# First layer's normed x transposed in one go ahead of its columns, x first in the load order, c read from two rows, other scheduling numbers

## The chip, the core and the metric

The kernel runs on one core of a Trainium2 chip. Its engines are named as the profile names them: PE (TensorE's matmuls; PEld its weight loads), DVE (VectorE), ACT (ScalarE), POOL (GpSimd, unused here), and SP (SyncE, which issues nearly all DMAs). The metric is the device time of one execution in microseconds (us); lower is better.

## What is computed

Two layers of an encoder over x (256 tokens x 2048 channels, float32), with a conditioning vector c of 2048 numbers:

```python
def hybrid_layer(x, c, ...):
    mod = (c @ w_ada + b_ada)[:, None, :]
    shift, scale, gate = jnp.split(mod, 3, axis=-1)
    h = rms_norm(x, g_pre) * (1 + scale) + shift
    z = h @ w_in                      # 2048 x 6144: u, g_pool, q, k, v, g_diff
    pool_out = multiscale_pool(u, w_pool, pool_scale) * jax.nn.silu(g_pool)
    q, k = apply_rope(q), apply_rope(k)
    att = rms_norm(diff_attention(q, k, v, lam), subln_g) * (1.0 - lam_init)
    diff_out = att * jax.nn.silu(g_diff)
    y = jnp.concatenate([pool_out, diff_out], axis=-1) @ w_out   # 2048 x 2048
    return x + (1 + gate) * rms_norm(y, g_post)
```

Everything is float32. Weights are 245 MB in all, read once.

## The kernel before

**Products.** The 256 tokens are two groups (st = 0, 1) of 128; the 2048 channels are 16 k tiles of 128, taken in pairs kp = 0..7. A *unit* is one 512 KB piece of w_in or w_out: two k tiles by 512 columns (one of the twelve column blocks nb of w_in). Most products split each float32 operand into a rounded part and a remainder: `whi` (ACT's CAST of the raw tile), `wlo` (DVE's subtraction), `hz` (both parts of h). A unit is then 12 matmuls. As k tiles of h become available one after the other, a column block is visited several times; at the end of a visit its sums are copied out to `z` and, at the next visit, back in to an accumulator bank.

**The start.** The modulation columns are needed before any h. DVE multiplies each 512 KB tile of w_ada (`adaz`, 128 channels by half of c) by c, which has been spread over all partitions (`cb`), and adds up along the row. Four such tiles give shift and scale of one k tile; three small steps write them to `AB`. c is spread by PE: `spread_c` multiplies a row of ones by c in four pieces (`psb<-cb,ones`), and ACT copies each to `cb`. Meanwhile x's two groups are squared and summed (`first_squares`), and `rms` gives each token's factor `ry`.

The first three units (group 1) are not split: full float32 products with the raw tiles (`accc<-rawz,halfz`), kp = 0 alone, in the order k0 of group 0, k0 of group 1, then k1 of both. Their h is made in `half_h`: ACT scales 256 columns of x by `ry`, PE transposes them (a matmul with the identity, `psb<-consts,halfz`), ACT applies `AB` and writes `halfz`. `half_h` also issues 18 dummy transposes (WARM) behind the first two. From the fourth unit on, the split products run without a pause: the main stream. For kp = 1..7 of the first layer `make_h` does the same as `half_h` when the k pair is due: two scalings, four transposes, four modulations from the PSUM bank, two subtractions.

**The order of the work.** The program is straight-line code for every engine, in an order that a planner sets while the kernel is built. Each part of the work is a task (`spawn`) with a due time; `Flow` keeps a model clock for each engine, with costs by operation (COST), by megabyte on the link (MB_US) and for landing (LANDING). `next_of` picks, for an engine, the task with the earliest due time that could start without idling; on PE a task with a due time counts as startable only SLACK us after its data is modelled ready. An engine executes its instructions strictly in this order, so an instruction that waits holds all behind it. `plan` fixes which unit follows which; ORDERS says which column block takes which place, RATE how many w_ada tiles are read per unit. The DMA issues wait on eight landing semaphores in turn, so at most eight loads are outstanding.

**Buffers.** PSUM has eight banks, four for sums (`accc`) and four others (`psb`); two of the second four hold the third first unit's sums (`accb`) through the start. `big` is a pool of 42 SBUF buffers of 4 KB per partition.

Of the kernel before, what the change touches and what calls it, by code (L numbers as in the profile page):

```python
# [129 lines left out]
class Flow:  # L130
# [10 lines left out]
    MB_US, LANDING, FIRST = 0.38, 2.4, 2.2  # L141
    COLD = (1.8, 4.0)

    SLACK = 1.5
# [66 lines left out]
    def next_of(self, k, asks):  # L211

        rows = []
        for t in asks:
            a = t.ask
            if a.dep is None:
                a.dep = self.depends(a)
            us = a.us + self.TABLE_US * bool(a.table and a.table[0] != self.table)
            due = t.due()
            slack = self.SLACK * (k == "tensor" and 0 < due < 1e8)  # L220
            rows.append((due, max(self.now[k], a.dep + slack), us, t))
# [29 lines left out]
    def turn(self, key, op, outs, ins, total, table):  # L251
# [8 lines left out]
        a.names = {r[0] for r in a.outs + a.ins} | {r[0] for _, r in a.also}  # L260
        a.dep, a.f32 = None, key == "tensor" and op == "matmul" and ins[-1].dtype == F32
# [143 lines left out]
class Kern:  # L405
# [169 lines left out]
    def run(self):  # L575
# [11 lines left out]
        self.rope_made = False  # L587
# [4 lines left out]
    def begin(self):  # L592
        nc, a, f = self.nc, self.a, self.f
        self.cb = self.const([P, D], "cb")
        nc.sync.dma_start(self.cb[0:1, :], a["c"])
        consts = self.const([P, HALF + P], "consts")
        nc.scalar.dma_start(consts, a["consts"])
        self.invf, self.ident = consts[:, :HALF], consts[:, HALF:]
        self.pos_i = self.const([P, NST], "posi", I32)
        nc.sync.dma_start(self.pos_i, a["positions"])  # L600
        self.cols = self.const([P, DEPTH, 89], "cols")
        nc.scalar.dma_start(self.cols, a["cols"])
        self.x = [self.const([P, D], f"x{st}_") for st in range(NST)]
# [4 lines left out]
        self.ones = self.const([1, P], "ones")  # L608
# [5 lines left out]
        self.arrived, self.squared = [False] * NST, False  # L614
        f.spawn(self.first_loads, -95.0)
        f.spawn(self.spread_c, -90.0)
# [13 lines left out]
        for l in range(DEPTH):  # L630
            f.spawn(lambda l=l: self.load_pool_weights(l))
            for kp in range(8):
                f.spawn(lambda l=l, kp=kp: self.make_h(l, kp), self.need_h(l, kp, 4.0))

    def first_loads(self):
# [13 lines left out]
        x(0)  # L649
# [11 lines left out]
    def spread_c(self):  # L661

        nc = self.nc
        for j in range(4):
            b, c = self.bank(), self.cb[:, j * 512 : (j + 1) * 512]
            nc.tensor.matmul(b, self.ones, c[0:1, :], start=True, stop=True)
            if j == 2:

                self.f.wait(lambda: self.squared)
            nc.scalar.copy(c, b)  # L670
            self.banks.give(b)
# [186 lines left out]
    def ada(self):  # L858

        v = self.nc.vector  # L860
        for e in self.adas:
# [9 lines left out]
            if i and 16 <= nt < 32 and (nt % 2 or not l and nt < 18):  # L871

                kt = nt - 16
                self.ab(l, kt if not l and kt < 2 else kt - 1, kt + 1)
# [4 lines left out]
    def ab(self, l, k0, k1):  # L879
# [5 lines left out]
        v.tensor_tensor(ab[:, 1], ab[:, 1], self.cols[:, l, 48 + k0 : 48 + k1], op=ALU.mult)  # L885

# [19 lines left out]
    def first_squares(self, st):  # L906
# [6 lines left out]
        if st:  # L913

            f.wait(lambda: self.made[0])
            more = self.big.take([P, D // 2], "junk")
            self.nc.vector.scalar_tensor_tensor(
                more, x[:, c[1]], self.ROOT**2, x[:, c[1]], op0=ALU.mult, op1=ALU.mult, accum_out=ss[:, st, 3:4]
            )
            self.big.give(more)  # L920
            f.wait(lambda: (0, 0) in self.h_whole)
            square(0)
        else:
            square(0), square(1)
# [3 lines left out]
        self.xr[0][st] = self.rms(ss[:, st, 2:5])  # L928
# [10 lines left out]
    def make_h(self, l, kp):  # L939
# [15 lines left out]
        f.wait(lambda: all(r is not None for r in self.xr[l]))  # L955
        xn = self.tmp.take([P, NST, S], "xn")
        for st in range(NST):
            self.scaled(xn[:, st, :], self.x[st][:, kp * S : (kp + 1) * S], self.xr[l][st])
# [524 lines left out]
```

## Time and profile before

| | us |
|---|---|
| median of 3 runs | 818.13 (816.19 to 821.13) |
| the profiled execution | 817.44 |
| its span, first to last instruction | 815.7 |
| PE busy in the span | 794.2 |
| first product of the first units | 15.84 |
| first product of the main stream | 31.25 |
| last product | 807.47 |

The span is 1.7 us shorter than the execution's time, which in turn is 0.7 us below the median. DVE is busy for 697.3 us, ACT for 545.8 us. The link moves 343 to 410 GB/s through the first 120 us, and less later. In the rows, a line gives the start, the duration, the engine, the source line, the operation, `out<-in` by tile names, the shape, and in brackets the idle time of the engine before it and what ended it. All work is recorded under line 125, a helper that records each operation, so the rows are read by tile names.

### The profile page before, as it was taken

What the parts mean: (1) busy time and instruction counts of PE and PEld (TensorE: products, weight loads), DVE (VectorE), ACT (ScalarE), POOL (GpSimd) and SP (SyncE); (2) the same over time, 40 slices, a digit from 0 to 9 for tenths busy, and PEclk for the clock granted to TensorE, in tenths of its full rate; (3) what the DMA queues carried; (4) which work ended last, traced back from release to release, by engine and by line L of the source; (5) the groups of instructions that cost most, each with busy time, mean ns of one, the idle gap of its engine ahead of it and who ended that gap; (6) DMA issues with size and microseconds to landing.
All of it is one profiled execution on the core that took longest, in us unless ns stands there. A gap on an engine that the chain in (4) does not pass through costs nothing. (4 is left out here: it accounts for less than half of the span.)

```text
span 815.7 us, 11813 instructions
## 1 busy us (share of the span) xinstructions
PE 794.2 (97%) x4032; PEld 658.5 (81%) x4032; DVE 697.3 (85%) x1232; ACT 545.8 (67%) x971; POOL 0.2 (0%) x4
## 2 busy tenths in 40 slices
PE   7899999999999999999999999999999999999995
PEld 3588789888997878788888889898898897787884
DVE  7889999998888899899999989878799889877924
ACT  4679998786655586886387557666656467677721
POOL 0000000000000000000000000000000000000000
PEclk9999999999999999999999999999999999999998
DMA  8999998999999877767999889999999895456302
GB/s 344 406 410 408 408 409 284 371 383 372 348 366 334 295 226 239 249 205 251 336 344 358 283 306 384 336 380 334 327 373 395 298 328 187 143 164 211 118 1 103
DMA packets 68382, 245.06 MB, mean 300 GB/s; under 512 B 7745, under 2 KB 8033, under 8 KB 68065
## 3 DMA queue, kind: packets, MB, share of 16 engines
q1 hardware_dynamic: 68034, 244.14, 82.6%
q8 instruction: 31, 0.51, 0.2%
q10 hardware_dynamic: 288, 0.17, 0.1%
q14 instruction: 29, 0.24, 0.1%
HBM read 242.17 MB, written 2.11 MB: 299 GB/s over the span
## 5 line engine op out<-in xcount | busy, mean ns | idle before, releaser
L125 PE MATMUL accc<-whiz,hz 128*128 128x512 f32 x1256 | 395.3, 393 | 1.2 <-ACT accc L125 0.7
L125 ACT CAST whiz<-rawz 128x1024 fp32r<-128x1024 f32 x253 | 260.1, 1052 | 104.6 <-DMA rawz<-in_w_in 66.9
L125 DVE TENSOR_TENSOR wloz<-rawz,whiz 128x1024 fp32r<-128x1024 f32 x253 | 303.5, 1219 | 12.3 <-ACT whiz L125 11.4
L125 PEld LDWEIGHTS accc<-whiz,hz 128*128 128x128 f32 x1256 | 234.7, 188 | 51.9 <-DVE hz L125 1.8
L125 DVE SCALAR_TENSOR_TENSOR adaz<-adaz,cb 128x1024 f32<-128x1024 f32 x192 | 231.2, 1219 | 35.3 <-DMA adaz<-in_w_ada 34.5
L125 PE MATMUL accc<-wloz,hz 128*128 128x512 f32 x628 | 245.5, 391 | 0.9 <-DVE wloz L125 0.9
L125 PE MATMUL accc<-whiz,catz 128*128 128x512 f32 x512 | 165.1, 398 | 1.0 <-ACT zz L125 1.0
L125 PEld LDWEIGHTS accc<-wloz,hz 128*128 128x128 f32 x628 | 118.0, 188 | 25.6 <-DVE wloz L125 1.7
L125 PEld LDWEIGHTS accc<-whiz,catz 128*128 128x128 f32 x512 | 94.6, 188 | 21.1 <-ACT zz L125 1.8
L125 PE MATMUL accc<-wloz,catz 128*128 128x512 f32 x256 | 101.6, 397 | 0.0
L125 ACT COPY accc<-zz 128x512 f32<-128x512 f32 x110 | 65.0, 591 | 29.0 <-DVE halfz L125 19.5
L125 ACT COPY zz<-accc 128x512 f32<-128x512 f32 x121 | 70.1, 585 | 14.4 <-PE accc L125 13.7
L125 PE MATMUL accc<-hz,whiz 128*128 128x256 f32 x512 | 72.1, 283 | 0.0
L125 PEld LDWEIGHTS accc<-hz,whiz 128*128 128x128 f32 x512 | 66.7, 192 | 0.8
L125 PEld LDWEIGHTS accc<-wloz,catz 128*128 128x128 f32 x256 | 48.1, 188 | 10.1 <-issue 0.7
L125 PE MATMUL accc<-hz,wloz 128*128 128x256 f32 x256 | 42.0, 284 | 0.0
L125 PEld LDWEIGHTS accc<-hz,wloz 128*128 128x128 f32 x256 | 35.6, 192 | 0.0
L125 ACT ACTIVATE sqj<-accc 128x512 bf16<-128x512 f32 x16 | 9.5, 597 | 37.9 <-PE accc L125 37.7
L125 PE MATMUL psb<-consts,halfz 128*128 128x128 f32 x176 | 30.5, 276 | 4.5 <-ACT halfz L125 2.4
L125 PEld LDWEIGHTS psb<-consts,halfz 128*128 128x128 f32 x176 | 22.1, 141 | 13.7 <-ACT halfz L125 4.9
L125 DVE TENSOR_TENSOR yz<-accc,Gz 128x512 f32<-128x512 f32 x16 | 10.9, 689 | 24.0 <-ACT sqj L125 23.8
L125 ACT ACTIVATE halfz<-psb,sm 128x128 f32<-128x128 f32 x64 | 26.3, 419 | 1.3 <-DVE sm L125 1.0
(112 smaller groups left out, 515.9 us busy)
## 6 DMA issues: line engine op xcount, KB each, us to landing
adaz<-in_w_ada SPq DMA_DIRECT2D x192, 512.0 KB, 7.2
rawz<-in_w_in SPq DMA_DIRECT2D x189, 512.0 KB, 7.8
rawz<-in_w_out SPq DMA_DIRECT2D x64, 512.0 KB, 4.0
x<-in_x SPq DMA_DIRECT2D x2, 1024.0 KB, 8.0
wpz<-in_w_pool SPq DMA_DIRECT2D x4, 512.0 KB, 6.6
Gz<-gate SPq DMA_DIRECT2D x4, 512.0 KB, 6.7
out<-x SPq DMA_DIRECT2D x8, 256.0 KB, 2.1
rawz<-in_w_in SPq DMA_DIRECT2D x6, 256.0 KB, 9.1
```

Of the source, the lines that this page charges most:

```text
L125: return f(*args, **kw)
```

## The change

It touches the start and the planner's numbers.

- SP issues x's first group first of all. The constants and the parameter columns (`cols`), two loads before, are one load of 338 columns, `consts`; c comes as two rows of 1024 at partitions 0 and 64 (`cz`); these and the positions go through ACT's queue.
- `spread_c` multiplies pairs: one piece of each half of c, from partitions 0 and 64. ACT copies one bank of a pair to `cb`, DVE the other.
- The second half of x's squares of group 0 is on DVE instead of ACT (`half_square`).
- New `turn_x`: once a group's `ry` is there, ACT scales columns 256 to 1023 and 1024 to 2047 of x (`xn`), PE transposes them, ACT copies them to SBUF (`xT`). For the first layer `make_h` then modulates from `xT`, with no scaling and no transpose of its own.
- 4 dummy transposes at the end of each `turn_x` instead of 18 behind the first two transposes.
- `ab_step` updates `AB` of the first two k tiles as each w_ada tile's sum arrives: one step after the last tile instead of three.
- Planner: LANDING 2.4 to 2.6, SLACK 1.5 to 1.2, RATE, ORDERS, and earlier due times for parts of attention and pooling. FED is 0, so the term that it multiplies is nothing.

```diff
-    MB_US, LANDING, FIRST = 0.38, 2.4, 2.2
+    MB_US, LANDING, FIRST = 0.38, 2.6, 2.2
-    SLACK = 1.5
+    SLACK = 1.2
+    FED = 0.0
-    WARM = 18
+    WARM = (4, 4)
-    RATE = {(0, 2): 0.82, (1, 2): 0.75, (0, 0): 0.92, (0, 1): 0.9, (1, 0): 0.8, (1, 1): 0.35}
-    ORDERS = [[10, 2, 3, 11, 6, 4, 0, 1, 7, 8, 5, 9], [2, 10, 0, 6, 11, 3, 4, 8, 5, 1, 7, 9]]
+    RATE = {(0, 2): 0.82, (1, 2): 0.85, (0, 0): 0.92, (0, 1): 0.9, (1, 0): 0.8, (1, 1): 0.4}
+    ORDERS = [[10, 2, 3, 4, 6, 0, 11, 1, 7, 8, 5, 9], [2, 10, 0, 6, 8, 4, 11, 3, 5, 1, 7, 9]]
...
+        nc.sync.dma_start(self.x[0], a["x"][0:P, :])
+        half = self.big.take([P, D // 2], "c")
+        for i, r in enumerate((0, 64)):
+            nc.scalar.dma_start(half[r : r + 1, :], a["c"][:, i * D // 2 : (i + 1) * D // 2])
+        consts = self.const([P, HALF + P + DEPTH * 89], "consts")
+        nc.scalar.dma_start(consts, a["consts"])
...
-        for j in range(4):
-            b, c = self.bank(), self.cb[:, j * 512 : (j + 1) * 512]
-            nc.tensor.matmul(b, self.ones, c[0:1, :], start=True, stop=True)
+        for j in range(2):
+            b = self.banks.take([P, NB], "ps", n=2)
+            for i, r in enumerate((0, 64)):
+                nc.tensor.matmul(b[i], self.ones[r : r + 1, :], half[r : r + 1, j * NB : (j + 1) * NB], start=True, stop=True)
+            nc.scalar.copy(self.cb[:, j * NB : (j + 1) * NB], b[0])
+            nc.vector.tensor_copy(self.cb[:, (2 + j) * NB : (3 + j) * NB], b[1])
...
+    def turn_x(self, st):
+        for c0, c1 in ((S, 4 * S), (4 * S, D)):
+            xn = self.big.take([P, 4 * S], "xn")
+            nc.scalar.activation(xn[:, : c1 - c0], self.x[st][:, c0:c1], AF.Copy, scale=self.xr[0][st])
+            for kp in {S: (1, 2), 4 * S: (4, 6)}[c0]:
...
+                    nc.tensor.transpose(b[:, i * P : (i + 1) * P], xn[:, k : k + P], self.ident)
...
+                nc.scalar.copy(o, b[:, : n * P].rearrange("p (i s) -> p i s", i=n))
...
+        self.warm(st)
...
-            f.spawn(one, self.need_cat(l, 4 + hp, 20.0 - h))
+            f.spawn(one, self.need_cat(l, 4 + hp, 22 - h))
```

Two places show how the instructions now stand. The first is the spreading of c. On DVE before, once the positions have been cast, the rotary steps (`halfz`) run through, and then the first w_ada tiles and the factor of x:

```order
L125 SCALAR_TENSOR_TENSOR halfz5_109<-halfz5_109 128x64 [waits DVE_49] x9
L125 TENSOR_SCALAR halfz8_118<-halfz5_109 128x64 [waits DVE_49]
L125 SCALAR_TENSOR_TENSOR adaz9_122,mod11_88<-adaz9_122,cb5_78 128x1024 [waits DMAHW5_49,DMAHW1_49,Activation_49]
L125 TENSOR_REDUCE rs22_196<-xss1_74 128x1 [waits Activation_49]
L125 CAST halfz5_109<-halfz8_118 128x64 [waits DVE_49]
L125 SCALAR_TENSOR_TENSOR halfz5_109<-halfz5_109 128x64 [waits DVE_49] x2
L125 RECIPROCAL ry23_197<-ry23_197 128x1 [waits Activation_49]
```

Now DVE has the copies to `cb` behind the positions' CAST and the first rotary steps (DMAHW5 is the positions' landing, PE the pair's product):

```order
L125 CAST posf19_123<-posi8_86 128x2 [waits DMAHW5_49]
L125 TENSOR_SCALAR halfz8_113<-consts7_84,posf19_123 128x32 [waits DVE_49]
L125 TENSOR_SCALAR halfz8_113<-consts7_84,posf19_123 128x32
L125 TENSOR_SCALAR halfz11_122<-halfz8_113 128x64 [waits DVE_49]
L125 CAST halfz8_113<-halfz11_122 128x64 [waits DVE_49]
L125 TENSOR_SCALAR halfz11_122<-halfz8_113 128x64 [waits DVE_49]
L125 CAST halfz8_113<-halfz11_122 128x64 [waits DVE_49]
L125 SCALAR_TENSOR_TENSOR halfz8_113<-halfz8_113 128x64 [waits DVE_49]
L125 SCALAR_TENSOR_TENSOR halfz8_113<-halfz8_113 128x64
L125 COPY cb9_88<-psb2_110 128x512 [waits PE_49]
L125 SCALAR_TENSOR_TENSOR halfz8_113<-halfz8_113 128x64 [waits DVE_49] x4
L125 COPY cb9_88<-psb6_175 128x512 [waits PE_49]
```

Behind these stand, in this order: the square of half of x's first group, a w_ada tile, the sum of the squares, a second tile, the four small steps to `ry` with one of `AB` among them, and two tiles with a step of `AB` behind each. On PE, before, the four spreading products waited for ACT alone:

```order
L125 MATMUL psb1_106<-cb5_78,ones15_96 128x512 [waits DMAHW1_49,DVE_49]
L125 MATMUL psb4_156<-cb5_78,ones15_96 128x512
L125 MATMUL psb5_173<-cb5_78,ones15_96 128x512 [waits Activation_49]
L125 MATMUL psb6_209<-cb5_78,ones15_96 128x512 [waits Activation_49]
L125 MATMUL psb7_233<-consts6_80,halfz8_118 128x128 [waits DMAHW0_49,Activation_49]
```

Now the second pair takes over the two banks of the first, and its second product waits for DVE's copy:

```order
L125 MATMUL psb1_109<-cz1_81,ones14_97 128x512 [waits DMAHW0_49,DVE_49]
L125 MATMUL psb2_110<-cz1_81,ones14_97 128x512 [waits DMAHW2_49]
L125 MATMUL psb5_174<-cz1_81,ones14_97 128x512 [waits Activation_49]
L125 MATMUL psb6_175<-cz1_81,ones14_97 128x512 [waits DVE_49]
L125 MATMUL psb7_231<-consts7_84,halfz11_122 128x128 [waits DMAHW4_49,Activation_49]
```

The second place is the first units' k1. On ACT before, the modulation of group 1's k0 (`halfz5<-psb9`) stood right behind that group's scaling (`halfz8<-x1`), and k1's first modulation behind it and the sine table:

```order
L125 ACTIVATE halfz5_109<-psb7_233,AB13_90 128x128 [waits DVE_49,PE_49]
L125 ACTIVATE junkz14_134,xss1_74<-x1_10_87 128x1024 [waits DMAHW2_49]
L125 ACTIVATE ry26_271<-rs25_270 128x1 [waits DVE_49]
L125 ACTIVATE halfz8_118<-x1_10_87,ry26_271 128x256 [waits DVE_49,Activation_49]
L125 ACTIVATE halfz5_109<-psb9_294,AB13_90 128x128 [waits PE_49]
L125 ACT_TABLE_LOAD
```

Now copies of `xT` and scalings of `xn` stand between (the sine table has gone to a place in the main stream):

```order
L125 ACTIVATE halfz8_113<-psb7_231,AB12_91 128x128 [waits DVE_49]
L125 ACTIVATE junkz15_135,xss1_74<-x1_6_79 128x1024 [waits DMAHW2_49]
L125 COPY xTz42_253<-psb9_243 128x4x128 [waits PE_49]
L125 ACTIVATE xnz43_262<-x0_5_78,ry22_202 128x1024 [waits DMAHW0_49]
L125 ACTIVATE ry26_257<-rs25_256 128x1 [waits DVE_49]
L125 COPY xTz44_278<-psb10_267 128x4x128 [waits PE_49,Activation_49]
L125 ACTIVATE halfz11_122<-x1_6_79,ry26_257 128x256 [waits DVE_49,Activation_49]
L125 COPY xTz45_290<-psb11_280 128x4x128 [waits PE_49]
L125 ACTIVATE xnz47_305<-x1_6_79,ry26_257 128x768
L125 ACTIVATE halfz8_113<-psb13_302,AB12_91 128x128 [waits PE_49]
L125 ACTIVATE halfz8_113<-psb7_231,AB12_91 128x128 [waits DVE_49]
```

On PE before, the six products of k1 followed each other, and then the main stream (`whiz`) began:

```order
L125 MATMUL accc1_112<-rawz1_103,halfz5_109 128x512 [waits DMAHW1_49,Activation_49]
L125 MATMUL accc2_113<-rawz1_103,halfz5_109 128x512 [waits Activation_49]
L125 MATMUL accc3_114<-rawz2_104,halfz5_109 128x512 [waits DMAHW2_49]
L125 MATMUL accc4_115<-rawz2_104,halfz5_109 128x512
L125 MATMUL accb2_116<-rawz3_105,halfz5_109 128x512 [waits DMAHW3_49]
L125 MATMUL accb3_117<-rawz3_105,halfz5_109 128x512
L125 MATMUL accc5_338<-whiz45_322,hz4_108 128x512 [waits DVE_49,Activation_49]
```

Now the transposes of x's second group stand among them:

```order
L125 MATMUL accc1_116<-rawz2_104,halfz8_113 128x512 [waits DMAHW1_49,Activation_49]
L125 MATMUL psb14_330<-consts7_84,xnz47_305 128x128 [waits Activation_49]
L125 MATMUL psb14_330<-consts7_84,xnz47_305 128x128
L125 MATMUL accc2_117<-rawz2_104,halfz8_113 128x512
L125 MATMUL psb15_341<-consts7_84,xnz47_305 128x128 [waits Activation_49]
L125 MATMUL psb15_341<-consts7_84,xnz47_305 128x128 x3
L125 MATMUL accc3_118<-rawz3_105,halfz8_113 128x512 [waits DMAHW2_49]
L125 MATMUL accc4_119<-rawz3_105,halfz8_113 128x512
L125 MATMUL accb3_120<-rawz4_106,halfz8_113 128x512 [waits DMAHW3_49]
L125 MATMUL psb16_359<-consts7_84,xnz52_352 128x128 [waits PE_49,Activation_49]
L125 MATMUL psb16_359<-consts7_84,xnz52_352 128x128 x3
```

Eight more transposes follow or stand beside the last product, and four dummies behind the third product of the main stream. Of the 28 transposes that `make_h` had in the main stream before, at seven places, none is left there.

More of the change, by code (lines that the diff above doesn't have):

```diff
@@ L219, in next_of @@
             due = t.due()
-            slack = self.SLACK * (k == "tensor" and 0 < due < 1e8)
+            slack = self.SLACK * (k == "tensor" and 0 < due < 1e8) + self.FED * (a.fed and due > 40)
             rows.append((due, max(self.now[k], a.dep + slack), us, t))
@@ L260, in turn @@
         a.names = {r[0] for r in a.outs + a.ins} | {r[0] for _, r in a.also}
+        a.fed = not a.dma and any(r[0].startswith(("ada", "raw")) for r in a.ins)
         a.dep, a.f32 = None, key == "tensor" and op == "matmul" and ins[-1].dtype == F32
@@ L915, in first_squares @@
             f.wait(lambda: self.made[0])
[L916 to L920, printed above, removed]
+            self.half_square(st)
             f.wait(lambda: (0, 0) in self.h_whole)
@@ L923, in first_squares @@
         else:
-            square(0), square(1)
+            f.wait(lambda: self.spread)
+            self.half_square(st), square(0)
             self.squared = True
@@ L954, in make_h @@
             return
[L955 to L958, printed above, removed]
-        b = self.bank()
-        for i in range(2):
-            for st in range(NST):
-                nc.tensor.transpose(b[:, i * S + st * P : i * S + (st + 1) * P], xn[:, st, i * P : (i + 1) * P], self.ident)
-        self.tmp.give(xn)
+        if l:
+            f.wait(lambda: all(r is not None for r in self.xr[l]))
+            xn = self.tmp.take([P, NST, S], "xn")
+            for st in range(NST):
+                self.scaled(xn[:, st, :], self.x[st][:, kp * S : (kp + 1) * S], self.xr[l][st])
+            bank = self.bank()
+            for i in range(2):
+                for st in range(NST):
+                    nc.tensor.transpose(bank[:, i * S + st * P : i * S + (st + 1) * P], xn[:, st, i * P : (i + 1) * P], self.ident)
+            self.tmp.give(xn)
+            b = bank.rearrange("p (i s) -> p i s", i=2)
+        else:
+            f.wait(lambda: all((kp, st) in self.turned_x for st in range(NST)))
+            b = self.xT[kp // 2][:, kp % 2 * 2 : kp % 2 * 2 + 2, :]
         hf = self.tmp.take([P, 2, S], "hf")
@@ L987, in half_h @@
         hf = self.tmp.take([P, 2, P], "hf") if whole is None else whole[:, :, c]
-        if whole is not None and not st:
-            d = self.bank()
-            for i in range(self.WARM):
-                nc.tensor.transpose(d[:, 0:P], self.ident, self.ident)
-            self.banks.give(d)
+        if whole is not None:
+            self.turned_x.add((kp, st))
         def first(i):
@@ L1020, in half_h, with warm @@
         self.used_whole(kp)
+    def warm(self, n):
+        d = self.bank()
+        for i in range(self.WARM[n]):
+            self.nc.tensor.transpose(d[:, 0:P], self.ident, self.ident)
+        self.banks.give(d)
     def used_whole(self, kp):
@@ L1471 @@
     }
+    names = ("b_ada", "g_pre", "g_post", "pool_scale", "subln_g")
+    host["consts"] = np.concatenate(host["consts"] + [np.concatenate([cols(i[k]) for k in names], axis=2).reshape(P, -1)], axis=1)
     host = {k: np.ascontiguousarray(v) for k, v in host.items()}
```

97 lines of the change are left out of this document (65 added, 32 removed).

## The prediction

> **What bounds the kernel now.** I began with the busy time by stages. The columns are the stretch, its length, the busy time of PE, of PE's weight loads, of DVE, ACT and POOL with their instructions, PE's granted clock (1 is full), the busy share of the DMA engines, and GB/s.
>
> ```profile
> 24.00:31.25 7.25, 6.55 (x12) 2.81 (x13) 5.63 (x12) 7.06 (x13) 0.00 (x0) 0.76 1.03 410
> 31.25:84.00 52.75, 51.88 (x275) 44.35 (x274) 48.81 (x72) 44.17 (x71) 0.00 (x0) 1.00 1.03 409
> 84.00:210.00 126.00, 125.81 (x611) 105.48 (x610) 116.79 (x177) 103.20 (x153) 0.00 (x0) 1.00 0.98 369
> 210.00:807.00 597.00, 592.45 (x3098) 497.36 (x3096) 503.66 (x897) 379.65 (x712) 0.00 (x0) 1.00 0.78 276
> ```
>
> From 31.25 on PE is the bound: it idles 0.9 us of 52.75, 0.2 of 126 and 4.6 of 597. So only three things count: when the main stream begins, how much PE has to do in it, and those idle pieces. The tail behind PE's last product holds the same work before and after, and I leave it as it is. PE's waits come next; a row gives who waited for whom, then the sum, the number and the longest.
>
> ```profile
> PE psb L125 <- ACT halfz L125: 2.4, 2, 2.0
> PE psb L125 <- DVE halfz L125: 2.1, 2, 1.2
> PE accc L125 <- ACT zz L125: 1.0, 2, 0.7
> PE accc L125 <- DVE wloz L125: 0.9, 1, 0.9
> PE accc L125 <- ACT accc L125: 0.7, 1, 0.7
> PE accc L125 <- DVE hz L125: 0.6, 2, 0.4
> ```
>
> In order of time, the 2.0 of the first row and the 0.7 of the third lie in the start, the 0.9 and 0.2 of the last row at 80 and 87 us; what is left, 2.1 + 0.4 + 0.3 + 0.7 + 0.4, some 3.8 us, lies behind 260 us. Last, PE's start:
>
> ```profile
> 2.68 7.16 PE L125 MATMUL psb<-cb,ones 1*128 1x512 f32 x8 [2.68 <-DMA cb<-in_c]
> ...
> 15.84 1.98 PE L125 MATMUL accc<-rawz,halfz 128*128 128x512 f32 x4
> 17.66 1.02 PE L125 MATMUL accb<-rawz,halfz 128*128 128x512 f32 x2
> ...
> 24.70 5.40 PE L125 MATMUL accc<-rawz,halfz 128*128 128x512 f32 x8 [2.32 <-ACT halfz L125]
> 29.94 1.88 PE L125 MATMUL accb<-rawz,halfz 128*128 128x512 f32 x4
> 31.25 0.80 PE L125 MATMUL accc<-whiz,hz 128*128 128x512 f32 x1
> ```
>
> A full float32 product is two passes, and four of them take 17.66 - 15.84 = 1.82, so 0.455 a pass. At 24.70 PE has waited 2.3 us for h of k1. From there twelve passes fill the 6.55 us to 31.25, 1.1 more than 12 x 0.455 = 5.46; the clock column has 0.76 for this stretch. So the start is bound by the last `AB` step of k1, and the main stream follows 6.55 us behind k1's first product.
>
> **The new start, step by step.** DVE sets `AB`, so I follow DVE.
>
> ```profile
> 4.10 0.16 DVE L125 CAST posf<-posi 128x2 f32<-128x2 int32 x1
> ...
> 5.72 2.70 DVE L125 SCALAR_TENSOR_TENSOR halfz<-halfz 128x64 f32<-128x64 f32 x11
> ...
> 11.13 1.22 DVE L125 SCALAR_TENSOR_TENSOR adaz<-adaz,cb 128x1024 f32<-128x1024 f32 x1
> 12.27 1.22 DVE L125 SCALAR_TENSOR_TENSOR adaz<-adaz,cb 128x1024 f32<-128x1024 f32 x1
> ...
> 14.88 0.16 DVE L125 TENSOR_TENSOR AB<-AB,b 128x2 f32<-128x2 f32 x1
> 15.07 0.16 DVE L125 TENSOR_TENSOR AB<-AB,cols 128x1 f32<-128x1 f32 x1
> 15.41 1.23 DVE L125 SCALAR_TENSOR_TENSOR junkz<-x 128x1024 f32<-128x1024 f32 x1
> ...
> 22.33 1.23 DVE L125 SCALAR_TENSOR_TENSOR adaz<-adaz,cb 128x1024 f32<-128x1024 f32 x1 [0.40 <-DMA adaz<-in_w_ada]
> 24.00 0.16 DVE L125 TENSOR_TENSOR AB<-AB,cols 128x1 f32<-128x1 f32 x1
> ...
> 30.14 0.69 DVE L125 COPY zz<-accc 128x512 f32<-128x512 f32 x1 [0.42 <-PE accc L125]
> ```
>
> `AB` was complete for k0 at 15.07 + 0.16 = 15.23 and for k1 at 24.16. A w_ada tile takes 1.15 us from start to start, a small step 0.2. DVE waited only 0.4 us for the last w_ada tile, so loads and DVE were nearly level.
>
> Now DVE's chain begins at the positions' CAST, with all of the rest queued behind it, and the positions are the last of four loads on ACT's queue, behind x's first group.
>
> ```profile
> 0.73 0.35 SPq L125 DMA_DIRECT2D cb<-in_c  x1
> ```
> ```profile
> cols<-in_cols ACTq DMA_DIRECT2D x1, 89.0 KB, 2.8
> ```
> ```profile
> DMA to landing us min/median/max: 5.3/8.0/10.7
> ```
>
> The first row is SP's first issue; the second ends with the time to landing; the third has the landing times of tile x's two loads. No row shows a small load behind x alone. Low: issued at about 1.5 like the second load of a queue and landing in 2.8 like `cols`, 4.3. High: behind the whole of x's first group, 0.73 + 5.3, and half a microsecond more, 6.5. I take 5.0, nearer to `cols`, which shared the last third of its way with x and still landed in 2.8; before it was 4.1.
>
> Then 1.62 (from 4.10 to 5.72) brings DVE to the first multiplying steps, two of them cost 2 x 2.70/11 = 0.5, so 7.1. Copy of the first bank to `cb` at 0.69: 7.8. Only now can the second pair's second product go, since it takes that bank. The price of such a product up to its reader is 2.08, from PE's 2.68 to ACT's first copy:
>
> ```profile
> 4.76 0.59 ACT L125 COPY cb<-psb 128x512 f32<-128x512 f32 x1 [1.65 <-PE psb L125]
> ...
> 15.69 1.04 ACT L125 ACTIVATE junkz<-x 128x1024 bf16<-128x1024 f32 x1
> ...
> 17.99 0.51 ACT L125 ACTIVATE halfz<-x,ry 128x256 f32<-128x256 f32 x1 [0.74 <-DVE ry L125]
> 19.03 0.46 ACT L125 ACTIVATE halfz<-psb,AB 128x128 f32<-128x128 f32 x1 [0.53 <-PE psb L125]
> 19.51 1.28 ACT L125 ACT_TABLE_LOAD   x1
> ```
>
> That gives 9.9, and 10.6 with DVE's second copy. The rest adds up from the rows above: the square of half of x, 1.23, 11.8; a tile, the sum, a tile, 2 x 1.15 + 0.15, 14.25; four small steps, 15.05; two tiles with a step behind each, 2 x (1.15 + 0.2). **k0's `AB` is complete at 17.75, 2.5 later than before.** Up to k1 DVE has two rotary steps (0.45), the square of group 1 (1.15), five small ones (1.2), four tiles (4.6) and six small steps (1.2), 8.6 in all: **26.35 against 24.16, 2.2 later.** All loads are in by then: before, the last of these eight tiles landed at 22.3. x leaving 0.8 earlier (it was SP's third issue) thus gains nothing, as DVE, not x, comes last.
>
> On ACT k0's modulation of group 1 is no longer next. From 17.75 + 0.46 = 18.2 on there stand the square of half of group 1 (1.04), three copies to `xT` (0.59 each, the copy to `cb` being of their shape), two scalings to `xn`, the scaling of k0 (0.51) and the small step to `ry` (0.2). No row has a scaling 768 or 1024 wide; 0.51 (256 wide) and 1.04 (the square, 1024 wide) bound them, and I take 0.8 and 1.04. That is 23.6; two waits for PE's transposes like the 0.53 above make 24.6, the modulation and the step to PE 25.3. Group 1's k0 on PE is six passes of 0.455, 2.73: **k1 starts on PE at 28.1 against 24.70, 3.4 later.** `AB` of k1, 26.35, is just covered by this. Then come the twelve passes and 14 transposes at 0.113 (next fence), 5.46 + 1.6 = 7.05 against 6.55. **The main stream starts 3.9 later, at 35.2.**
>
> **What the main stream saves.** One of the seven places with four transposes:
>
> ```profile
> 51.29 0.39 PE L125 MATMUL accc<-wloz,hz 128*128 128x512 f32 x1
> 51.97 0.39 PE L125 MATMUL accc<-wloz,hz 128*128 128x512 f32 x1
> 52.20 0.27 PE L125 MATMUL psb<-consts,halfz 128*128 128x128 f32 x1
> ...
> 53.10 0.40 PE L125 MATMUL accc<-wloz,hz 128*128 128x512 f32 x1
> ...
> 80.36 0.50 PE L125 MATMUL accc<-wloz,hz 128*128 128x512 f32 x1 [0.87 <-DVE wloz L125]
> ```
>
> The first transpose is shown, three more stand behind it. With them the two products around are 1.13 apart, and the two products ahead of them, with none between, 0.68: 0.45 for a place, 0.113 for a transpose, 3.15 for seven. The four dummies in the main stream cost 0.45. The waits of 0.87 and 0.19 for DVE at 80 and 87 us should close: PE comes some 3.9 later, DVE's queue only 2.2. The removed scalings, on ACT and not waited for, give PE nothing. Attention now has four more table loads, 4 x 1.28 = 5.1 on ACT, which is idle 217 of 597 us there; I cost them at nothing, and at up to 5.1 if each met a product waiting. SLACK lowered by 0.3 can add that to each of the three places where PE already waits for rotated or normalized h behind 260 us, +0.9; other orders and earlier due times can take up to the 3.8 away. With both signs open and no row to choose by, I take 0, the value of nearly all of 3098 products there.
>
> **The sum**, against the profiled execution of 817.44: +3.9 + 0.45 - 3.15 - 1.06 = +0.2, 817.6. The median of the three runs is 0.7 above that execution, so **818.3**. With the positions at 4.3 it is 817.7, at 6.5 it is 819.8.
>
> **The rivals.**
>
> *Earlier due times work.* The 3.8 us behind 260 close. For it: the two biggest, 1.2 and 0.8, are transposes that wait for DVE's rotary steps, and just these tasks get earlier due times. Against it: DVE is 84% busy there, and something earlier for one is later for another. 818.3 - 3.8 = 814.5, and 813.9 with an early landing.
>
> *ACT becomes the bound at 31 to 84 us.* ACT has 8.6 us idle there.
>
> ```profile
> 49.02 0.91 ACT L125 ACTIVATE halfz<-x,ry 128x256 f32<-128x256 f32 x2
> ```
>
> Into that stretch come the last copies to `xT` (2.0), the last scaling (1.04), the sine table and its two uses (1.9), and three copies to `z` that DVE had (1.65); the scalings of two pairs (2 x 0.91) go: +4.7. The split tile is cast on ACT, subtracted on DVE, then used, and the wait at 80.36 shows the lead of this over PE at nothing. ACT's work on h moved back by as much as PE's, so the later start gives it no lead. It decides from the point where the 4.7 find no idle time on ACT ahead of the tightest product. At its full price 818.3 + 4.7 = 823.0, slower. Against it stand the 8.6 idle.
>
> *PE's clock falls once more.* After the 2.3 us wait at 24.70 it fell, and the twelve passes took 1.1 longer. In the new start PE has done group 0's k0 by about 21.2 (18.5 + 2.73) and gets group 1's at 25.3, with 14 transposes (1.6) between: 2.5 us idle in pieces. If that is enough, 818.3 + 1.1 = 819.4. The Trainium skill, "TensorE: Matmul & The Clock Gate", Part 1, puts the fall to half rate at an idle window of about 3.4 us and full rate at as long a busy one; by that rule no gap here would drop it. The trace does not agree on the fall, as 2.3 us were enough here, and the measurement decides.
>
> *The change does what its order suggests.* k1 stays bound by its loads, which come 0.8 earlier: k1 at 23.9, main stream at 23.9 + 7.05 = 30.95, so -0.3 in place of +3.9: 814.1. Against it stands DVE's chain above, which would have to begin some 3 us sooner than I find; CAST at 1 us is before any landing in this trace.
>
> **How the numbers follow.** My forecast, 816.8 to 819.8, gets 0.37; the earlier due times 0.29, half of it below 814.0; the ACT bound 0.17; the clock 0.10; the earlier loads 0.07, nearly all below 814.0 as soon as any later wait closes as well. 0.5%, 4.1 us, is about what a measurement can tell from no change: faster is below 814.0, 0.14 + 0.06 = 0.20; slower is above 822.2, 0.15 of the ACT bound's 0.17 and 0.01 of a lowered clock with a late landing; 0.64 is left between. The range goes from 813.5 to 823.0, which leaves out the joined gains below, and above it an ACT bound with a late landing.
>
> **What would show it.** Right: the CAST of the positions at about 5 and DVE's second copy to `cb` at about 10; k0's `AB` at 17.7; k1's first product at about 28 and the first `whiz` product at about 35; no transposes between 40 and 210; no wait for `wloz` at 80 to 90. Wrong: k1's first product below 26, so that DVE or ACT has less in the way than I count; PE waiting for ACT's casts at 35 to 90; or a sum of waits behind 260 us below 2 or over 6 in place of 3.8.

## The result, and the profile after

| | before | after |
|---|---|---|
| median of 6 runs | 817.16 | 825.15 (823.13 to 831.27) |
| ratio | | 1.0119, 95% interval 1.0083 to 1.0156 |
| the profiled execution, span | 817.44, 815.7 | 829.33, 827.5 |
| first product of the main stream | 31.25 | 42.03 |
| from there to the 1050th product into `accc` | 204.70 | 200.71 |
| from that to the last product | 571.42 | 576.43 |
| behind the last product | 8.3 | 8.4 |

The change makes the kernel slower, by 8.0 us at the median. The table's lower part adds up to the 11.9 us between the two profiled executions: the main stream starts 10.8 later, wins 4.0 in its first 200 us, and loses 5.0 in the rest. (The 1050 products are counted from the first of the main stream. Behind them PE has the same 2902 instructions left in both kernels; the times are counted out of the traces.) The profiled execution is 4.2 above the median of its kernel, so these pieces are at the upper end: three executions below that have late loads, DVE's copies and `turn_x` as well begin the main stream at 39.7 to 40.1.

The start is read on PE first. A row gives start, duration, engine, line, operation, tiles, shape, count, and in brackets the idle time ahead and what ended it.

```profile
5.84 2.08 PE L125 MATMUL psb<-cz,ones 1*128 1x512 f32 x4 [1.27 <-DMA cz<-in_c]
13.13 2.07 PE L125 MATMUL psb<-cz,ones 1*128 1x512 f32 x2 [5.21 <-DVE cb L125]
20.61 0.69 PE L125 MATMUL psb<-consts,halfz 128*128 128x128 f32 x2 [5.40 <-ACT halfz L125]
...
23.49 3.62 PE L125 MATMUL accc<-rawz,halfz 128*128 128x512 f32 x4
26.91 1.64 PE L125 MATMUL accb<-rawz,halfz 128*128 128x512 f32 x2
...
32.75 1.98 PE L125 MATMUL accc<-rawz,halfz 128*128 128x512 f32 x4 [0.55 <-ACT halfz L125]
...
35.43 1.02 PE L125 MATMUL accc<-rawz,halfz 128*128 128x512 f32 x2
...
42.03 0.47 PE L125 MATMUL accc<-whiz,hz 128*128 128x512 f32 x1
```

The last product that spreads c waits 5.2 us for DVE's copy, as the prediction had it, but starts at 13.13 and not at 7.8. Group 0's k0 (23.49 to 28.4) takes (26.91 - 23.49) / 4 = 0.855 a pass, where group 1's k0 (32.75) and the k0 of both groups in the kernel before took half of that: PE ran at half rate here. ACT in turn waited for PE; this row of its timeline is the first copy to `xT` behind those products:

```profile
29.08 0.59 ACT L125 COPY xTz<-psb 128x512 f32<-128x512 f32 x1 [3.18 <-PE psb L125]
```

DVE's timeline and the loads' rows (the last number is the time from issue to landing) say where it begins:

```profile
9.27 0.18 DVE L125 COPY b<-consts 128x32 f32<-128x32 f32 x1 [8.02 <-DMA consts<-in_consts]
...
10.57 0.17 DVE L125 CAST posf<-posi 128x2 f32<-128x2 int32 x1 [0.90 <-DMA posi<-in_positions]
...
15.24 0.69 DVE L125 COPY cb<-psb 128x512 f32<-128x512 f32 x1 [1.25 <-PE psb L125]
...
22.53 0.22 DVE L125 SCALAR_TENSOR_TENSOR AB<-mod,most,consts 128x1 f32<-128x1 f32 x1
...
30.99 0.22 DVE L125 SCALAR_TENSOR_TENSOR AB<-mod,most,consts 128x1 f32<-128x1 f32 x1
```
```profile
consts<-in_consts ACTq DMA_DIRECT2D x1, 169.0 KB, 7.7
...
posi<-in_positions ACTq DMA_DIRECT2D x1, 1.0 KB, 8.6
```

DVE did nothing for 8 us: the constants took 7.7 us to land and the positions, 1 KB, 8.6. Before, `cols` took 2.8 and the CAST stood at 4.1.

In the main stream PE is busy without a gap to 84 us (windows, columns as in the prediction), so ACT did not become the bound there:

```profile
42.03:84.00 41.97, 41.97 (x224) 36.12 (x223) 37.93 (x56) 39.53 (x62) 0.00 (x0) 1.00 0.97 369
```

PE's longer waits behind 300 us stand at other places than before:

```profile
316.68 1.20 PE L125 MATMUL psb<-band,zz 128*128 128x144 f32 x8 [0.42 <-ACT halfz L125]
318.88 1.99 PE L125 MATMUL psb<-halfz,wpz 128*128 128x256 f32 x8 [0.56 <-ACT halfz L125]
323.39 0.50 PE L125 MATMUL accc<-whiz,catz 128*128 128x512 f32 x1 [0.88 <-DVE halfz L125]
...
426.38 0.51 PE L125 MATMUL accc<-whiz,hz 128*128 128x512 f32 x1 [2.25 <-ACT hz L125]
```
```profile
424.93 1.04 ACT L125 CAST whiz<-rawz 128x1024 fp32r<-128x1024 f32 x1 [2.71 <-DMA rawz<-in_w_in]
425.88 0.45 ACT L125 ACTIVATE hz<-psb,AB 128x128 fp32r<-128x128 f32 x1
```
```profile
424.00:427.50 3.50, 1.25 (x5) 0.69 (x5) 0.90 (x3) 2.57 (x6) 0.00 (x0) 1.00 0.99 384
427.50:431.00 3.50, 3.50 (x10) 2.70 (x9) 3.35 (x7) 3.50 (x9) 0.00 (x0) 0.51 1.04 421
```

The first fence is PE, the second ACT at 425: PE waits for layer 1's first h, whose modulation stands on ACT behind a CAST, and the CAST waits 2.7 us for its load. The third fence adds what such a wait costs besides: in the 3.5 us behind it the clock column shows 0.51, some 1.7 us more.

The waits are the smaller part of what is lost in the rest. The stretch behind the 1050 products, before and after:

```profile
235.95:807.38 571.43, 566.88 (x2902) 472.31 (x2900) 481.83 (x870) 364.77 (x695) 0.00 (x0) 1.00 0.77 272
```
```profile
242.74:819.17 576.43, 570.64 (x2902) 472.88 (x2900) 486.01 (x874) 369.00 (x698) 0.00 (x0) 1.00 0.77 271
```

PE idles 5.8 us in place of 4.6, 1.2 more, and is busy 3.8 us longer with as many instructions. 1.7 of the 3.8 is the lowered clock; for the other 2.1 no run gives the cause.

### The profile page after: what moved, and what is told of

Read it like the earlier page. It is cut to its first block, busy times and chain, and to the rows that moved or that the text cites. A ratio compares the mean times of both kernels' runs of the same rounds, so it can differ in the third digit from the quotient of the medians.

```text
span 827.5 us, 11764 instructions
## 1 busy us (share of the span) xinstructions
PE 795.9 (96%) x4022; PEld 656.5 (79%) x4022; DVE 699.8 (85%) x1232; ACT 552.4 (67%) x973; POOL 0.2 (0%) x4
## 4 chain that ended last, share of the span: by engine, by line
PE 86%; DMA 6%; ACT 3%; DVE 3%; issue 1%; DVEq 0%; SPq 0%; ACTq 0%
PE accc L125 78%; PE psb L125 8%; DMA adaz<-in_w_ada 3%; DMA rawz<-in_w_in 3%; ACT whiz L125 1%; ACT zz L125 1%; DVE adaz L125 1%; ACT accc L125 1%; DVE wloz L125 1%; PE accb L125 0%; DVE halfz L125 0%; ACT halfz L125 0%; DVE x L125 0%; ACT xTz L125 0%; ACT hz L125 0%
## 5 line engine op out<-in xcount | busy, mean ns | idle before, releaser
L125 PE MATMUL accc<-whiz,catz 128*128 128x512 f32 x512 | 167.4, 400 | 0.9 <-DVE halfz L125 0.9
L125 PEld LDWEIGHTS accc<-whiz,catz 128*128 128x128 f32 x512 | 95.1, 188 | 23.1 <-issue 2.0
L125 ACT COPY accc<-zz 128x512 f32<-128x512 f32 x106 | 62.6, 591 | 21.6 <-DVE halfz L125 17.2
L125 PE MATMUL psb<-consts,halfz 128*128 128x128 f32 x148 | 26.0, 278 | 6.8 <-ACT halfz L125 6.7
L125 PEld LDWEIGHTS psb<-consts,halfz 128*128 128x128 f32 x148 | 18.5, 141 | 14.8 <-ACT halfz L125 9.7
L125 ACT ACTIVATE halfz<-psb,sm 128x128 f32<-128x128 f32 (+1 forms) x64 | 26.5, 421 | 4.8 <-DVE sm L125 4.2
```

The source lines that it names most:

```text
L125: return f(*args, **kw)
```

## The experiments

All of them compute the whole result. "Same order" means that every engine's other instructions stand as in the kernel named: the planner is told the old issue, and only the instruction itself is issued otherwise. Ratios are against the kernel before, with their 95% interval; "main" is the first product of the main stream in the profiled execution (31.25 before, 42.03 after), and "rest" the time from the 1050th product on (571.4 and 576.4).

### The small loads

The changed kernel in its own order, but issued as SP: c, positions, c, x; ACT: constants.

```diff
-        nc.sync.dma_start(self.x[0], a["x"][0:P, :])
-        (c, c, consts, positions on nc.scalar)
+        for eng, i in ((nc.sync, 1), (nc.scalar, 3), (nc.sync, 4), (nc.sync, 2), (nc.sync, 0)):
+            eng.eng.dma_start(*late[i])
```

> The changed kernel with one thing undone: c, the positions and the constants are issued ahead of x again (c and positions on SP, constants on ACT's queue); every engine's order of all other work stays that of the changed kernel. Theory A (the small loads behind x arrive late and hold DVE): CAST of the positions at 4 to 5 us in place of 10.6, first product of the main stream at 36 to 37 in place of 42.0, time 819 to 820. Rival B (the new order on DVE and ACT alone is what costs): CAST early, but the main stream still behind 40, time over 823.

Measured: 820.45, ratio 1.0032 (1.0008 to 1.0056), main 33.39. DVE and the loads:

```profile
3.07 0.18 DVE L125 COPY b<-consts 128x32 f32<-128x32 f32 x1 [1.82 <-DMA consts<-in_consts]
...
3.39 0.16 DVE L125 CAST posf<-posi 128x2 f32<-128x2 int32 x1
```
```profile
consts<-in_consts ACTq DMA_DIRECT2D x1, 169.0 KB, 2.3
...
posi<-in_positions SPq DMA_DIRECT2D x1, 1.0 KB, 2.1
```

The same bytes land in 2.3 and 2.1 us when x is issued behind them, the CAST stands 7.2 earlier, and main 8.6 earlier: theory A, and by more than I had expected of it (36 to 37). Against the 39.7 to 40.1 of the other executions with late loads it is some 6.5 earlier. The time falls by 4.7 at the median. This execution is the worst of its kernel (826.31), with a rest of 582.1, so its later waits are no guide; the same rest is 576.1 in the kernel with dummies below.

Is it the place in the queue, or what shares the link? The positions were put first on ACT's queue, x first on SP as in the change:

> The changed kernel with the positions first and the constants last on ACT's queue, x first on SP as it is. Theory S (each small packet queues on its DMA engine behind the big packets of x and w_ada, wherever its load stands in its queue): positions land 4 us or more behind their issue, constants 7.5 or more. Rival Q (a load only waits for those ahead of it on its own queue): positions land within 2.5 us of their issue. The time is no test here, as DVE needs the constants ahead of the CAST: 824 to 828 by both.

```profile
consts<-in_consts ACTq DMA_DIRECT2D x1, 169.0 KB, 7.5
...
posi<-in_positions ACTq DMA_DIRECT2D x1, 1.0 KB, 5.4
```

With nothing ahead of them on their queue the positions still take 5.4 us, theory S; being fourth added 3.2 more. (The time, 826.41, is that of a single run.) The packets on the two queues show how. q1 is SP's queue and q10 ACT's; a row gives packets, MB, and the time the packets took as a share of 16 engines. First this kernel from 2.1 to 5.1 us, then the changed kernel from 2.2 to 5.2, where no row for q10 is printed:

```profile
q1 hardware_dynamic: 114, 0.91, 77.7%
q10 hardware_dynamic: 114, 0.00, 2.1%
```
```profile
q1 hardware_dynamic: 164, 1.11, 92.1%
```

With the positions first, their rows of 8 bytes and x's rows of 8 KB go out one for one, and the last row of the positions starts at 5.57, where x's last starts at 5.27. In the changed kernel nothing of ACT's queue moves while x does: the second half of c, second on that queue, starts at 5.24, when x's last row ends; the constants follow from 5.30 and the positions from 7.58, both in turns with the w_ada tiles. Why that half of c stood still so long, and did not take its turn, was not settled. The Trainium skill, "DMA: Bandwidth & Descriptors", Queues, rings and completion order, says that each DMA engine takes turns between queues packet by packet, draining a whole packet of some 9 to 17 descriptors before it switches. The trace agrees on the turns but not on their size: the 114 packets of each queue above are single rows, one of the positions and one of x by turns.

### The chain on DVE

All four copies to `cb` on ACT, same order:

```diff
-            nc.vector.tensor_copy(self.cb[:, (2 + j) * NB : (3 + j) * NB], b[1])
+            nc.scalar.eng.copy(o, b[1])
```

> The changed kernel with all four copies to cb on ACT (both copies of DVE moved there, nothing else reordered, loads late as in the changed kernel). If the second pair's wait for DVE's copy is on the path: cb complete by 10 in place of 15.9, DVE's square of x at 13.3 in place of 15.9, main stream at 39 to 39.7 in place of 42.0, time 822 to 823. Rival (DVE's late begin alone counts, its copies are covered): main stream within 0.7 of 42.0, time 824.5 to 826.

Measured: 823.39, ratio 1.0056 (1.0037 to 1.0075), main 38.93. PE, then DVE:

```profile
8.03 2.07 PE L125 MATMUL psb<-cz,ones 1*128 1x512 f32 x2 [0.67 <-ACT cb L678]
```
```profile
12.88 1.22 DVE L125 SCALAR_TENSOR_TENSOR junkz<-x 128x1024 f32<-128x1024 f32 x1
```

The last spreading product starts at 8.03 in place of 13.13, DVE's square of x at 12.88 in place of 15.85. The loads landed 0.55 earlier here (CAST at 10.02), so the copies and their wait are worth 2.4 of these 3.0 us: the step is on the path. Main follows: 28.9 behind the CAST in place of 31.5.

### PE's clock

24 dummies behind the last spreading product, same order, on the changed kernel and with the small loads first:

> The changed kernel with 24 dummy transposes added behind the last product that spreads c, in time in which PE waits; the order of all else is kept. Theory C (PE ran the first k0 products at half rate because no dummies raise its clock ahead of them, and ACT waits behind these): passes of group 0's k0 0.43 apart in place of 0.855, main stream 2 to 3 us earlier (39 to 40), time 822 to 823. Rival D (those products are hidden behind the wait for AB and the second group's squares): passes at 0.43, main stream within 0.5 of 42.0, time unchanged at 825.

> Both edits of the two kernels before. If A and C hold and add up: main stream at 33.5 to 34.5, time 816.5 to 817.5. If C only counts while DVE is late: main stream as with the loads alone, 36 to 37, time 819 to 820.

Measured: 825.02, ratio 1.0081 (1.0051 to 1.0111), main 40.09, and 820.56, ratio 1.0026 (0.9999 to 1.0053), main 34.17: neither time is told apart from the kernel without dummies. PE with the late loads:

```profile
14.34 4.73 PE L679 MATMUL psb<-consts 128*128 128x128 f32 x24
...
22.49 3.25 PE L125 MATMUL accc<-rawz,halfz 128*128 128x512 f32 x4
25.58 1.02 PE L125 MATMUL accb<-rawz,halfz 128*128 128x512 f32 x2
```

The dummies ended too early. The clock's record has full rate from 18.24 to 21.66 and half rate again to 25.07, so the first three of the six passes of group 0's k0 still ran slowly, and the edit alone does not decide between C and D.

The executions together do. In the nine with `turn_x` and the new spreading, it is 2.85 to 4.27 us from the start of the first pass of group 0's k0 to that of the sixth, by how many ran at half rate:

| execution | first to sixth pass of group 0's k0 | sixth pass to first product of k1 |
|---|---|---|
| positions first | 2.85 | 7.48 |
| small loads first | 2.92 | 7.47 |
| old numbers (below) | 3.10 | 7.47 |
| small loads first, SLACK 1.35 (below) | 3.27 | 7.48 |
| 24 dummies | 3.52 | 7.47 |
| 24 dummies, small loads first | 3.57 | 7.48 |
| small loads first, SLACK 1.1 (below) | 3.75 | 7.47 |
| copies on ACT | 4.26 | 7.53 |
| changed kernel | 4.27 | 7.67 |

k1 begins 7.5 to 7.7 us behind the sixth pass, however late that is, so these passes are on the path, theory C: at full rate they would take 5 x 0.43 = 2.15, and the changed kernel lost 2.1 us of its start here. The time with dummies did not show it, as they won back only 0.75 of that.

A test that hit the clock was made on the kernel with `turn_x` and the new numbers only (below), where group 1's k0 ran at half rate. 7 dummies stand ahead of each of the three batches of transposes for which PE waits there, same order:

> The kernel with turn_x and the new numbers, with 7 dummy transposes put in front of each of the three batches of transposes for which PE waited 0.7 to 0.9 us each ahead of the second group's k0; the order of all else is kept. If the clock falls because PE is busy for too little of some 3.4 us there: passes of the second group's k0 0.43 apart in place of 0.85, main stream 1.7 to 2.5 earlier than 36.2, 817.5 to 818.5. If half rate is not reached by gaps under 1 us (as the page's idle window of 3.4 us would have it) and something else slows these passes: passes still 0.85 apart, main stream at 36 to 37.5, 820 to 821.

PE without and with them:

```profile
25.83 3.43 PE L125 MATMUL accc<-rawz,halfz 128*128 128x512 f32 x4 [0.55 <-ACT halfz L125]
```
```profile
26.61 1.98 PE L125 MATMUL accc<-rawz,halfz 128*128 128x512 f32 x4 [0.55 <-ACT halfz L125]
```

The four passes take 1.98 in place of 3.43 and the clock does not fall. But the dummies themselves put the products 0.8 later, main moves from 36.24 to 35.57, and the time stays (820.67, ratio 1.0045, 1.0015 to 1.0075, against 1.0023, 0.9999 to 1.0048). The clock is thus a real cost, but raising it by dummies won little here. The Trainium skill, "TensorE: Matmul & The Clock Gate", Part 1, puts the fall at an idle window of about 3.4 us. The trace does not agree that the window must be idle: no gap here was over 0.9 us, and transposes ran between.

### turn_x

The kernel before with the new numbers and `turn_x`, everything else of the start as before:

> The kernel before with the new numbers and turn_x (no dummies behind it, the 18 of before kept); loads, spreading of c, squares and AB steps as before. By the prediction's working: main stream 2.5 to 3.5 behind that of the new numbers alone (29.6), so 32 to 33, and 3.2 less to do in it: 814 to 815. Rival (turn_x is hidden in the start): main stream at 29.6 to 30.3, 811 to 812. Rival (the plan of the second half turns worse with it, a wait of 1 us or more at layer 1's start): 816 to 819.

Measured: 819.90, ratio 1.0023 (0.9999 to 1.0048), main 36.24, against 814.49 and 29.59 without `turn_x` (next part): 5.4 lost, above all three ranges. Then the change without `turn_x` (transposes in `make_h` and 18 dummies in `half_h` as before), with the small loads first and, in the same order, late:

```diff
-        f.due(-5.2 + st)
-        self.turn_x(st)
```

> The changed kernel without turn_x (transposes in make_h and 18 dummies as before) and with c, positions and constants ahead of x. Theory: turn_x is what is left of the start's loss (33.4 against 31.25) and what the plan loses behind 200 us: main stream at 29.5 to 30.5, rest behind the 1050th product 566 to 571 us as in the kernels without turn_x and with the new numbers, 813.5 to 816. If the new spreading, squares and AB steps cost of themselves: main stream at 31.5 or later, 817 or more.

> The changed kernel without turn_x only; x first, small loads late. If the late small loads cost the same with and without turn_x: main stream 7 to 8.6 later than in the run before (37 to 39), time 820.5 to 823. If they only cost because turn_x stands behind them: main stream by 34, 817 or less.

Measured: 814.99, ratio 0.9973 (0.9947 to 0.9999), main 29.38; and 820.12, ratio 1.0030 (1.0002 to 1.0057), main 35.88. PE of the first of them:

```profile
24.53 3.70 PE L125 MATMUL accc<-rawz,halfz 128*128 128x512 f32 x8
28.07 1.88 PE L125 MATMUL accb<-rawz,halfz 128*128 128x512 f32 x4
29.38 0.79 PE L125 MATMUL accc<-whiz,hz 128*128 128x512 f32 x1
```

k1 now follows k0 without a wait and at full rate. The new spreading, squares and `AB` steps cost nothing of themselves, and gain nothing that can be told from the 814.49 of the new numbers alone. The four kernels make a square:

| median; main; rest | small loads late | small loads first |
|---|---|---|
| with `turn_x` | 825.15; 42.0; 576.4 | 820.45; 33.4; 582.1 |
| without | 820.12; 35.9; 568.5 | 814.99; 29.4; 569.7 |

By the medians late loads cost 4.7 and 5.1, and `turn_x` with its change of dummies costs 5.0 and 5.5: the two add up, as far as can be told, since the median of the kernel before itself lay between 817.2 and 818.1 in the groups of runs that these come from. Main and rest are those of one execution each. `turn_x` gives back 4.0 to 4.5 in the first 200 us of the main stream (200.7 against 204.8 and 205.3), as it should, but puts main 4.0 to 6.2 later and goes with a rest that is longer by 8 and 12 (the 12 in an execution that is the worst of its kernel), by 5.7 in the kernel with the old start. There the clock fell in neither stretch, and the 5.7 are 2.7 of waits and 3.0 in which PE is busy longer with the same 2902 instructions.

### The planner's numbers

The kernel before with the new numbers, and with three parts of them:

> The kernel before with only the planner's numbers of the change (LANDING, SLACK, RATE, ORDERS and the due times); loads, spreading of c, dummies and transposes as before. Neutral: main stream at 31.0 to 31.6, time 816 to 818. If the numbers cost (the wait of 2.2 us at 426 and the lower clock behind it in the changed kernel are theirs): 819 to 821. If earlier due times help: 813 to 815.

> The kernel before with only the earlier due times (attention, pooling, h, copies to the accumulators). If these alone bring the gain of the new numbers, as the rival of the prediction has it: the waits of 1.2 and 0.8 us at 262 to 265 gone, 814 to 815. If the orders or SLACK bring it: 817 to 819, with 3 to 4 us of waits behind 260 us.

> The kernel before with only ORDERS and RATE. If the order of the column blocks brings the gain: 814 to 815. If the due times bring it: 817 to 819.

> The kernel before with only SLACK 1.2 and LANDING 2.6. If these bring the gain: 814 to 815. By the prediction's bound (a smaller SLACK adds up to 0.9 us of waits): 818 to 819. No effect: 817 to 818.

| kernel before with | median | ratio (interval) | main | rest |
|---|---|---|---|---|
| all the new numbers | 814.49 | 0.9956 (0.9937 to 0.9974) | 29.59 | 566.8 |
| due times | 825.26 | 1.0108 (1.0067 to 1.0148) | 32.09 | 581.0 |
| ORDERS, RATE | 818.79 | 1.0022 (1.0004 to 1.0040) | 32.33 | 571.0 |
| SLACK, LANDING | 823.23 | 1.0075 (1.0047 to 1.0103) | 29.90 | 576.8 |

Together they have the lowest median of this study and beat both kernels (the 814.99 above is not told apart from it): the waits for DVE's rotary steps at 262 and 265 are gone, most others too (PE idles 1.0 us in the rest in place of 4.6), and of PE's waits in the main stream these are the longest left:

```profile
PE accc L125 <- DVE hz L125: 0.6, 2, 0.4
PE accc L125 <- DVE wloz L125: 0.5, 1, 0.5
PE accc L125 <- ACT catz L125: 0.3, 1, 0.3
```

Each part alone is slower than before (ORDERS and RATE only just), so no part carries the gain; it is one plan that fits. In the column for main the clock plays in: PE waits 1.6 to 2.3 us for k1 in all four and in the kernel before, and where half rate followed (before, due times, ORDERS with RATE) the main stream begins 6.55 behind k1's first product, elsewhere 4.85. The reverse, the changed kernel with the old numbers:

> The changed kernel with the planner's numbers of before (LANDING, SLACK, RATE, ORDERS, due times). If the numbers are worth as much here as on the kernel before (3.6 us): 828 to 830. If their gain is lost in the changed kernel (the wait of 2 us at layer 1's start, in a plan that holds the copies xT): 823 to 826, with waits behind 260 us of 3 to 5 us as in the kernel before.

Measured: 828.87, ratio 1.0124 (1.0083 to 1.0165), an interval that nearly covers the changed kernel's own: undecided. How touchy the plan is, four kernels with only SLACK moved show:

> The kernel before with the new numbers, SLACK 1.25 in place of 1.2; no work is added or removed. If the plan behind 200 us is a matter of chance in its numbers: another time by 2 us or more than 814.5, in waits behind 200 us. If the numbers carry a gain of their own: 813.5 to 815.5.

> The same with SLACK 1.35. Chance in the plan: 816 to 822. A gain of the numbers' own: 813.5 to 816.

> The changed kernel with c, positions and constants ahead of x, SLACK 1.1 in place of 1.2. If what is lost behind 200 us is chance in the plan and not turn_x: another time by 2 us or more than 820.4, either way, with the main stream's start at 33 to 34. If turn_x itself loses it (its tiles held, its copies): waits behind 200 us as before, 819.5 to 821.5.

> The same with SLACK 1.35: chance in the plan, a time 2 us or more away from 820.4; turn_x itself, 819.5 to 821.5.

On the kernel before with the new numbers: 816.97, ratio 1.0000 (0.9980 to 1.0021), rest 568.4, and 816.47, ratio 0.9986 (0.9966 to 1.0006), rest 570.5. So 0.05 in one number costs most of the gain. On the changed kernel with the small loads first: 822.89, ratio 1.0059 (1.0031 to 1.0087), rest 574.4, and 820.64, ratio 1.0048 (1.0026 to 1.0071), rest 575.9: neither is told apart from the 1.0032 (1.0008 to 1.0056) with SLACK 1.2, and neither is near the kernels without `turn_x`. In the ten kernels with `turn_x` and the new numbers or SLACK near them the rest is 572.6 to 582.1, in the five without it 566.8 to 570.5. All ten have the same three waits as the changed kernel between 308 and 324 us (pooling's `band` and `wpz` products waiting for ACT, and a product behind them for DVE). Of the five, three have no wait between 250 and 400 us, and the two with another SLACK have one or two at other places. So a small move of one number cost the kernel without `turn_x` 2.0 and 2.5 us at the median, and `turn_x` brings these waits besides. They sum to 0.8 to 1.9 us, less than half of what the rest grew by; the longer busy time of PE goes with them, 2.2 of its 3.0 us (old start, with against without `turn_x`) in the stretch from the 1050th product to about 344 us. Why the planner sets pooling so when the transposes are gone, and why PE is slower there, was not settled.

## Why the prediction was wrong, by its own steps

**The step that failed** is the landing of the positions: "Low: ... 4.3. High: behind the whole of x's first group, 0.73 + 5.3, and half a microsecond more, 6.5. I take 5.0, nearer to `cols`". It landed at 10.57, outside both ends. Two things in it were wrong. `cols` had been issued ahead of x, so its 2.8 says nothing of a load behind x. And the high end let only x pass. For x alone it was right: put first on ACT's queue, the positions landed at 0.72 + 5.4 = 6.1. It left out the three loads ahead of them on their own queue, of which the constants' 169 KB took turns with the w_ada tiles; that put the landing 4.4 later still. The chain behind it was sized well:

| us behind the CAST | predicted | after | small loads first |
|---|---|---|---|
| CAST | 5.0 | 10.57 | 3.39 |
| DVE's second copy to `cb` | +4.9 | +4.7 | +4.8 |
| `AB` of k0 complete | +12.75 | +12.2 | +12.3 |
| `AB` of k1 complete | +21.35 | +20.6 | +21.0 |
| first product of k1 | +23.1 | +24.9 | +23.4 |
| main stream | +30.2 | +31.5 | +30.0 |

With the CAST at 3.39 the working gives a main stream at 33.6; 33.39 was measured. In that execution the first two passes of k0 still ran slowly, and from k1 to the main stream it took 6.6 where 7.05 was summed, so the last 0.2 are a fair fit and some luck.

**The dummies.** I priced them only by the time they take (+0.45) and the transposes likewise. In the kernel before the 18 of them stand ahead of k0, and the clock's record rises at 15.04, just ahead of k0's first product at 15.84; in the changed kernel it rises at 28.13, in the last pass of group 0's k0. This costs 2.1 us there, in the table the 1.8 by which k1 comes later than predicted. The rival of a lowered clock had the clock fall ahead of group 1's k0, at 1.1 us; instead it had not yet risen for group 0's.

**What the main stream saves** came out right in sum: 3.15 + 1.06 - 0.45 = 3.8 forecast, 4.0 measured by the 1050th product. The terms partly make up for each other. PE's busy time fell by 3.4 (203.6 to 200.25) where 2.7 was forecast; of the waits for DVE, which should all have closed, 0.46 us for `wloz` at 87.7 stayed.

**The later waits at nothing** was wrong by 5.0. The text had both ends open (+0.9 to -3.8) and took 0; neither end holds the +5. Only 1.2 of it is idle time: new waits came where the old plan had none, and old ones went. 1.7 is half rate behind one new wait, and 2.1 PE's longer busy time, for which the prediction had no term. The 3.8 was also misread: the 0.7 us of the row for `zz` stands at 696.6 us and not in the start, so PE's waits behind 260 us were 4.6.

**The rivals.** The earlier due times were named with 814.5, and the new numbers on the kernel before give 814.49 and close the waits at 262 and 265; but not through the due times, which alone give 825.3, and not in the changed kernel. That the two numbers agree is luck. ACT as the bound at 31 to 84 us did not come: PE idles 0.0 there. The earlier x gained nothing, since DVE comes last; the price of its place was on the other loads. A slower kernel had 0.16: 0.15 for ACT as the bound, which did not come, and 0.01 for a lowered clock with a late landing, which came near to what happened, though with a landing at 6.5 at most.

## What to carry to other kernels

Small loads that an engine's whole queue waits for go out ahead of the megabytes: here, for 1 KB of positions, c and 169 KB of constants, that was worth 5 us. The bound for a late one is everything issued before it on all queues, not the landing of the nearest row. Work taken out of a stream that is never idle pays in full; put into the start, where each step waits for the one before, it cost more than it had saved. Where a planner sets the order, a removed or added piece is measured together with a small change of the planner's numbers on either side, since those alone moved the kernel before between 814.5 and 825.3 us.

## What the runs showed of the hardware that was not expected

- Half rate comes and goes in pieces of 3.413 us by the clock's record (427.5 to 430.9 in the changed kernel, 21.66 to 25.07 in the one with 24 dummies, 25.37 to 28.78 in the one with `turn_x` alone). One wait of 2.25 us was enough for it, and so were three of 0.7 to 0.9 us with ten transposes between. Nor does such a wait always bring it: ahead of k1, waits of 2.00 and 1.99 us were followed by half rate (ORDERS with RATE; SLACK 1.35 on the kernel before), one of 2.00 was not (SLACK 1.25), nor was one of 2.50 at 299 us in that same execution.
- PE began at half rate: the passes of the changed kernel show it by their duration (0.855 in place of 0.43) though the clock column reads 1.00 there, its first record being the rise at 28.1 us in the changed kernel and at 15.0 in the one before.
- Two loads on different queues went out row by row in turn: 114 rows of 8 bytes and 114 rows of 8 KB in the same 3 us, so 1 KB took 5.4 us beside 1 MB (positions first), against 2.1 ahead of it.
